# A hybrid decoder layer on one core: the front's work on PE in another order, with added matmuls of ones, and each visit's first weights traced one visit ahead

## The chip, the core and the metric

The kernel runs on one core of a Trainium2 chip. The metric is the device time of one execution in microseconds (us), as the median of 3 runs. The engines are called as in the profile: PE (TensorE, with PEld for its weight loads), DVE (VectorE), ACT (ScalarE), POOL (GpSimd) and SP (SyncE, which here issues the loads).

## What is computed

One decoder layer over 256 tokens of width 2048 in fp32, conditioned by a vector `c`. The first stage, where the change lies, is this part of the reference:

```python
mod = jax.nn.silu(c) @ w_ada[l] + b_ada[l]
shift1, scale1, gate1, shift2, scale2, gate2 = jnp.split(mod, 6, axis=-1)
h = modulate(rms_norm(x, g_norm1[l]), shift1, scale1)
p = h @ w_in[l]
```

`rms_norm` divides by the root mean square of a token and multiplies by a gain; `modulate` is h (1 + scale) + shift. Behind `p` come a retention branch and an HGRN2 branch, a merge, a second norm, a gated convolutional feed-forward and a final norm; none of them is changed.

## The kernel before

**Tiles.** Tokens are 256 columns, channels are 16 k-tiles of 128 partitions. `x` lies transposed in four tiles `xT` of four k-tiles each. A weight load (`load`, L161) brings two k-tiles by 512 columns (128x1024, 512 KB) or one (128x512) on SP's queue into one of 11 `raw` buffers. ACT rounds it to fp32r (`wh`, L176, in `upper`), DVE subtracts to get the rest (`wl`, L181, in `rest`), and PE forms a product of three: `wh` with the upper half of the activation `hT`, `wh` with its lower half, and `wl` with the upper half. `mm_cols` (L221, L222, L225) does it with weights as the stationary operand in passes of 256 columns, `mm_rows` (L205, L206, L210) with the activation as stationary in passes of 512 columns. Of the twelve column groups (`ATT`) four go by columns, eight by rows.

**The conditioning.** `mod` isn't a matmul: a row of `w_ada` transposed and its bias (2049 numbers on each of 128 partitions) is multiplied with silu(c), held on all partitions in `sc`, and summed along the row on DVE (`ada_dot`, L465, two dots of 1024 and 1025 for a scale or a shift). `scale_shift` makes from these the scale (L476, L477) and the shift (L479) of one k-tile on ACT; `modulated` makes `hT` of it (L389 and L393 on ACT, L394 on DVE). For the front `c` is loaded as two rows, spread over the partitions by four fp32 matmuls with a row of ones (L303, one active row), and passes through Silu on ACT. The squares of `x` (L372, L376) are added on DVE (L377, L378), summed over channels by matmuls of one column (L342), and a square root, a reciprocal (L352) and two matmuls (L356) give `rx`, the inverse norm of each token on all partitions; `times` (L455) multiplies it into `xT`.

**The front** (`run`, L840 to L875): for k-tile 0, then 1, the first four groups (`FIRST`, all by columns) are multiplied, with weights of one k-tile each. Groups 0 and 1 (`RESIDENT`) keep their PSUM banks until their last k-tile; the others are copied out (`take`, L835 by ACT when new, L837 added by DVE).

**Visits** (L891 on). After the front the program goes round the twelve groups. A visit brings a group as far as the k-tiles of `hT` then due: `have`, which grows by one with every `ADA_EVERY` (11) units of work, `LAG` units late. `finish` emits the steps of the due k-tiles, `products` walks through the visit's weights two k-tiles at a time (`pieces`) and lets background generators (`pump`) emit the next k-tiles' dots between. So a visit's weights are traced within the visit, and its `take` behind them.

**Order.** Up to `self.ordered = False` (L868) pinned instructions (`pin`) keep the program's order on their engine; later the scheduler of the tile layer orders each engine's instructions, which then run strictly in that order. The small attention work and the tables of sine and cosine (`trig`, L527 to L529) are spread over the visits as background.

## Time and profile before

| what | value |
|---|---|
| median of 3 runs | 1501.31 us (1500.99 to 1501.91) |
| the profiled execution's own time | 1501.3 us |
| its span, first to last instruction | 1499.5 us |
| instructions in it | 22668 |
| PE, DVE, ACT busy | 99%, 81%, 56% of the span |
| mean granted TensorE clock | 0.999 |
| read from HBM | 382.11 MB, 256 GB/s over the span |

A span of nearly the whole time means that little lies around it. Busy shares are averages over stages; what a change in a stage is worth is read there: which engine waits, for what, and what ended the wait. In rows of the timeline the first number is the start, the second the duration, both in us; `x4` are four merged instructions, and brackets tell the idle time before. A matmul's duration has its drain in it, so the pace of PE is read from start to start. An fp32 matmul stands as two passes, an fp32r one as a single pass, shown as f32.

### The profile page before, as it was taken

The numbers are of one execution on the slowest core, as the hardware profiler recorded it, in microseconds if no ns is written. First come the engines' busy times: TensorE is split into PE (matmuls) and PEld (weight loads), VectorE is DVE, ScalarE is ACT, GpSimd is POOL, SyncE is SP. The second block draws the span as 40 slices with busy tenths as digits, with TensorE's granted clock in tenths as the row PEclk, the third lists the DMA queues.
The fourth block names the chain that finished last, engine by engine and source line by source line (L and its number), as shares of the span: only waits on it lengthen the run. The fifth ranks groups of instructions, "written<-read, shape, count | busy, mean of one in ns | idle before, by whom it ended". The sixth has DMA issues, their size and how long they took to land.

```text
span 1499.5 us, 22668 instructions
## 1 busy us (share of the span) xinstructions
PE 1482.9 (99%) x8466; PEld 1268.5 (85%) x8466; DVE 1208.5 (81%) x1647; ACT 838.1 (56%) x1210; POOL 4.0 (0%) x8
## 2 busy tenths in 40 slices
PE   8999999999999999999999999999999999999997
PEld 6889899888888888888888888888888888888886
DVE  7899997998999877898978778777777769455684
ACT  5745456767775644455466556555555558344342
POOL 0000000000000000000000000000000000000000
PEclk9999999999999999999999999999999999999999
DMA  9999997778887899989847777777777666666551
GB/s 373 365 341 346 316 335 257 267 252 277 278 280 262 286 295 328 317 295 356 307 126 244 245 236 233 234 238 237 228 250 230 221 190 207 195 210 214 177 186 56
DMA packets 110994, 385.71 MB, mean 257 GB/s; under 512 B 12802, under 2 KB 13346, under 8 KB 110884
## 3 DMA queue, kind: packets, MB, share of 16 engines
q1 hardware_dynamic: 110016, 383.14, 76.6%
q8 instruction: 66, 1.08, 0.3%
q10 hardware_dynamic: 868, 1.13, 0.2%
q14 instruction: 44, 0.36, 0.1%
HBM read 382.11 MB, written 2.11 MB: 256 GB/s over the span
## 4 chain that ended last, share of the span: by engine, by line
PE 94%; DVE 2%; DMA 1%; ACT 1%; issue 1%; SPq 0%; DVEq 0%; ACTq 0%
PE pg L205 13%; PE pg L210 13%; PE pg L206 13%; PE po L1134 11%; PE pg L1134 11%; PE po L1136 5%; PE pg L1136 5%; PE pg L232 4%; PE po L205 3%; PE po L210 3%; PE po L206 3%; PE pg L235 2%; PE pg L222 1%; PE pg L221 1%; PE pg L225 1%; PE po L225 1%
## 5 line engine op out<-in xcount | busy, mean ns | idle before, releaser
L181 DVE TENSOR_TENSOR wl<-raw,wh 128x1024 fp32r<-128x1024 f32 (+1 forms) x536 | 632.8, 1191 | 222.7 <-ACT wh L176 214.1
L176 ACT ACTIVATE wh<-raw 128x1024 fp32r<-128x1024 f32 (+1 forms) x536 | 547.2, 1032 | 471.0 <-PE pg L206 196.9
L465 DVE SCALAR_TENSOR_TENSOR raw<-raw,sc 128x1024 f32<-128x1024 f32 x192 | 233.7, 1221 | 0.0
L205 PE MATMUL pg<-wh,hT 128*128 128x512 f32 x512 | 202.3, 395 | 0.9 <-DVE p L837 0.6
L206 PE MATMUL pg<-wh,hT 128*128 128x512 f32 x512 | 199.8, 390 | 0.0
L1134 PE MATMUL po<-h2T,wh 128*128 128x512 f32 x704 | 175.8, 392 | 0.0
L1134 PE MATMUL pg<-h2T,wh 128*128 128x512 f32 x688 | 172.1, 392 | 0.0
L1134 PEld LDWEIGHTS po<-h2T,wh 128*128 128x128 f32 x704 | 125.6, 188 | 21.7
L1134 PEld LDWEIGHTS pg<-h2T,wh 128*128 128x128 f32 x688 | 122.8, 188 | 21.3
L210 PE MATMUL pg<-wl,hT 128*128 128x512 f32 x512 | 138.4, 390 | 0.1
L205 PEld LDWEIGHTS pg<-wh,hT 128*128 128x128 f32 x512 | 96.1, 188 | 21.5 <-ACT f L586 1.0
L210 PEld LDWEIGHTS pg<-wl,hT 128*128 128x128 f32 x512 | 96.0, 188 | 20.6 <-DVE wl L181 0.4
L206 PEld LDWEIGHTS pg<-wh,hT 128*128 128x128 f32 x512 | 96.2, 188 | 19.6 <-DVE hT L394 0.3
L1136 PEld LDWEIGHTS po<-h2T,wl 128*128 128x128 f32 x704 | 93.4, 188 | 7.5
L1136 PEld LDWEIGHTS pg<-h2T,wl 128*128 128x128 f32 x688 | 91.4, 188 | 7.3
L1136 PE MATMUL po<-h2T,wl 128*128 128x256 f32 x704 | 94.5, 277 | 0.0
L1136 PE MATMUL pg<-h2T,wl 128*128 128x256 f32 x688 | 92.5, 277 | 0.0
L206 PE MATMUL pg<-wh,gs 128*128 128x512 f32 x176 | 68.6, 390 | 0.0
L205 PE MATMUL pg<-wh,gs 128*128 128x512 f32 x176 | 68.5, 389 | 0.0
L205 PE MATMUL po<-wh,gs 128*128 128x512 f32 x176 | 68.5, 389 | 0.0
L206 PE MATMUL po<-wh,gs 128*128 128x512 f32 x176 | 68.5, 389 | 0.0
L1147 ACT ACTIVATE u<-uy,convw 128x256 f32<-128x256 f32 x88 | 52.4, 595 | 28.7 <-DVE uy L1145 28.4
(255 smaller groups left out, 2023.9 us busy)
## 6 DMA issues: line engine op xcount, KB each, us to landing
raw<-in_wup SPq DMA_DIRECT2D x176, 512.0 KB, 4.6
raw<-in_wdown SPq DMA_DIRECT2D x88, 512.0 KB, 4.2
raw<-in_wa SPq DMA_DIRECT2D x80, 512.0 KB, 5.8
raw<-in_ada SPq DMA_DIRECT2D x64, 512.5 KB, 5.7
raw<-in_ada SPq DMA_DIRECT2D x64, 512.0 KB, 5.4
raw<-in_wab SPq DMA_DIRECT2D x64, 512.0 KB, 5.4
raw<-in_gate SPq DMA_DIRECT2D x32, 512.5 KB, 5.0
raw<-in_wk SPq DMA_DIRECT2D x32, 512.0 KB, 5.2
```

The costliest lines, as they stand in the source:

```text
L176: self.pin(self.nc.scalar.activation(wh, raw, AF.Copy))
L181: self.last = self.nc.vector.tensor_tensor(wl, raw, wh.bitcast(F32), ALU.subtract)
L205: nc.tensor.matmul(ps[t], lhsT=act[:, hi], rhs=wh, start=first and i == 0, stop=False)
L206: nc.tensor.matmul(ps[t], lhsT=act[:, lo], rhs=wh, start=False, stop=False)
L210: nc.tensor.matmul(ps[t], lhsT=act[:, hi], rhs=wl, start=False, stop=last and i == len(items) - 1)
L225: nc.tensor.matmul(outs[j], lhsT=wl[:, cs[j]], rhs=act[:, :T], start=False, stop=last and i == len(items) - 1, skip_group_check=True)
L232: nc.tensor.matmul(ps[z], lhsT=wh[:, z * P : (z + 1) * P], rhs=act, start=first and i == 0, stop=False)
L235: nc.tensor.matmul(ps[z][:, :T], lhsT=wl[:, z * P : (z + 1) * P], rhs=act[:, :T], start=False, stop=last and i == len(items) - 1)
L465: dot = self.pin(nc.vector.scalar_tensor_tensor(raw[:, 0, :], raw[:, 0, :], 1.0, self.sc[:, u * GW : u * GW + w], ALU.mult, ALU.mult, accu ...
L1134: self.pin(nc.tensor.matmul(ps[z], lhsT=wh[:, z * P : (z + 1) * P], rhs=act, start=kt == 0, stop=False, skip_group_check=bool(begun)))
L1136: nc.tensor.matmul(ps[z][:, :T], lhsT=wl[:, z * P : (z + 1) * P], rhs=act[:, :T], start=False, stop=kt == KT - 1, skip_group_check=bool(be ...
L1147: nc.scalar.activation(u, y, AF.Identity, bias=w[3], scale=w[2])
```

## The change

It rewrites the front, and moves the tracing of weights in the visits:

- `c` is loaded as 16 rows of 128 behind `ident`, turned by one transpose into a column `col`, passed through Silu once, and spread over the partitions by 16 fp32 matmuls of 128x128 (`spread`). The Silu of four row tiles becomes a Copy, and the table for the square root is loaded ahead of the squares.
- `idle` adds 21 fp32 matmuls of ones with ones, in four places (9, 1, 2 and 9), written to a PSUM tile that nothing reads.
- The last tile of squares is shared by ACT and DVE and is summed on PE without the adds on DVE.
- For k-tiles 0 and 1 the shift's dots are cut in three (1024, 512, 513). `opening` computes x times scale plus the first part on ACT, `summed` adds the other two parts on DVE; for k-tile 1 `summed` runs twice, once into the fp32r upper half.
- For k-tile 0 groups 0 and 1 multiply the loaded fp32 weights with the fp32 activation directly (`mm_plain`, four fp32 matmuls for each), without the split. For k-tile 1 `mm_apart` runs all products with the upper half first, then those with the lower half, then `wl`, over both groups.
- The first piece of visit 4 is traced in the front, and that of each later visit (`early`) before the `take` of the visit ahead of it. The plan of visits is made beforehand (`visits`). The takes of groups 2 and 3 come later, and `LAG` is 2.

```diff
-LAG = 1
+LAG = 2
...
+    def mm_plain(self, ps, w, h):
+        for j in range(4):
+            out = ps[j // 2][:, j % 2 * T : (j % 2 + 1) * T]
+            self.pin(self.nc.tensor.matmul(out, lhsT=w[:, j * P : (j + 1) * P], rhs=h, start=j % 2 == 0, stop=False, skip_group_check=True))
...
+    def mm_apart(self, pss, pieces, act):
+        nc = self.nc
+        n = range(len(pss))
+        for pick, cols in ((0, slice(0, T)), (0, slice(T, 2 * T)), (1, slice(0, T))):
+            for i in n:
+                for j in range(4):
+                    out = pss[i][j // 2][:, j % 2 * T : (j % 2 + 1) * T]
+                    w = pieces[i][pick][:, 0, j * P : (j + 1) * P]
+                    self.pin(nc.tensor.matmul(out, lhsT=w, rhs=act[:, cols], start=False, stop=False, skip_group_check=True))
...
+    def idle(self, n):
+        ps = self.pg()[0]
+        for _ in range(n):
+            self.pin(self.nc.tensor.matmul(ps[:, :P], lhsT=self.ones, rhs=self.ones, start=True, stop=True))
...
+        for step in begun or self.pieces(src[:, k0 : k0 + kts, :], kts, gain, shift):
...
-        rows = [self.blk([1, GW], name="crow") for _ in range(2)]
-        for u, row in enumerate(rows):
-            nc.scalar.dma_start(out=row, in_=a["c"][:, u * GW : (u + 1) * GW])
-        self.small_loads(nc.scalar, ("ident", "gn1"))
-        for u in range(4):
-            at = slice(u * G, (u + 1) * G)
-            ps = self.po()
-            nc.tensor.matmul(ps, lhsT=self.ones[0:1, :], rhs=rows[u // 2][:, u % 2 * G : (u % 2 + 1) * G], start=True, stop=True)
-            self.silu.append((self.sc[:, at], ps))
+        self.small_loads(nc.scalar, ("ident",))
+        row = self.blk([KT, P], name="crow")
+        self.pin(nc.scalar.dma_start(out=row, in_=a["c"]))
+        self.small_loads(nc.scalar, ("gn1",))
+        self.idle(9)
+        ps = self.po()[:, :KT]
+        self.pin(nc.tensor.transpose(ps, row, self.ident[:KT, :KT]))
+        self.idle(1)
+        col = self.small([P, KT], name="col", bufs=1)
+        self.pin(nc.scalar.activation(col, ps, AF.Silu))
+        self.sqrt_table()
+        self.col = col
+        for u in range(2):
+            self.spread(u)
+    def spread(self, u):
+        ps = self.po()
+        for i in range(4):
+            k = 4 * u + i
+            self.pin(self.nc.tensor.matmul(ps[:, i * P : (i + 1) * P], lhsT=self.col[:, k : k + 1].to_broadcast([P, P]), rhs=self.ident, start=True, stop=True))
+        self.silu.append((self.sc[:, u * G : (u + 1) * G], ps))
...
+        self.idle(2)
...
+        self.idle(9)
...
+        ps = self.po()[:, :NT]
...
             if i == 0:
                 self.pin(nc.vector.tensor_tensor(z, x, x, ALU.mult))
+            elif i < 3:
+                self.pin(nc.scalar.activation(z, x, AF.Square))
+                self.pin(nc.scalar.activation(*self.silu.pop(0), AF.Copy))
             else:
-                if i < 3:
-                    self.pin(nc.scalar.activation(*self.silu.pop(0), AF.Silu))
-                self.pin(nc.scalar.activation(z, x, AF.Square))
-            self.pin(nc.vector.tensor_tensor(z[:, :2, :], z[:, :2, :], z[:, 2:, :], ALU.add))
-            self.pin(nc.vector.tensor_tensor(z[:, 0, :], z[:, 0, :], z[:, 1, :], ALU.add))
-            parts.append(z[:, 0, :])
+                self.pin(nc.scalar.activation(z[:, :2, :], x[:, :2, :], AF.Square))
+                self.pin(nc.vector.tensor_tensor(z[:, 2:, :], x[:, 2:, :], x[:, 2:, :], ALU.mult))
+            if i < 3:
+                self.pin(nc.vector.tensor_tensor(z[:, :2, :], z[:, :2, :], z[:, 2:, :], ALU.add))
+                self.pin(nc.vector.tensor_tensor(z[:, 0, :], z[:, 0, :], z[:, 1, :], ALU.add))
+            self.sums(ps, [z[:, j, :] for j in range(1 if i < 3 else 4)], i == 0, i == 3)
+            if i == 0:
+                for u in (2, 3):
+                    self.spread(u)
...
-        if k == 0:
-            self.pin(self.nc.vector.tensor_scalar(h, x, sc[:, k : k + 1], sh[:, k : k + 1], ALU.mult, ALU.add))
-        else:
-            self.pin(act(h, x, AF.Identity, bias=sh[:, k : k + 1], scale=sc[:, k : k + 1]))
+        self.pin(act(h, x, AF.Identity, bias=sh[:, k : k + 1], scale=sc[:, k : k + 1]))
...
+    def ada_dot(self, src, cuts=(0, GW, D + 1)):
...
+        self.dots = part = self.small([P, len(cuts) - 1], name=f"dot{len(cuts)}", bufs=6 if len(cuts) == 3 else 2)
+        for u, (at, to) in enumerate(zip(cuts, cuts[1:])):
+            raw = self.load(src[:, at:to], 1, to - at)
+            dot = self.pin(nc.vector.scalar_tensor_tensor(raw[:, 0, :], raw[:, 0, :], 1.0, self.sc[:, at:to], ALU.mult, ALU.mult, accum_out=part[:, u : u + 1]))
...
+        if fine:
+            yield from self.ada_dot(self.a[name][k, 1], (0, GW, GW + G, D + 1))
+            return
...
+        def summed(dst, z, part):
+            self.pin(nc.vector.tensor_scalar(dst, z, part[:, 1:2], part[:, 2:3], ALU.add, ALU.add))
+        def first(k):
+            return self.scale_shift("ada1", k, s1, t1, self.gn1, fine=True)
+        def opening(k):
+            z = self.s1([P, T], name="z")
+            self.pin(nc.scalar.activation(z, self.xT[0][:, k, :], AF.Identity, bias=self.dots[:, 0:1], scale=s1[:, k : k + 1]))
+            return z
+        ada = [None, None, *(ada1(k) for k in range(2, KT))]
+        gen = first(0)
+        for _ in range(2):
+            next(gen)
...
+        next(gen)
+        self.times(0, 1, rx)
+        self.pin(nc.scalar.activation(rx_sb, rx, AF.Copy))
+        z = opening(0)
+        for _ in gen:
+            pass
+        h = self.s1([P, T], name="h")
+        summed(h, z, self.dots)
+        ps = {0: self.po2(), 1: self.po2()}
+        hT[0] = self.blk([P, 2, 2 * T], F32R, name="hT")
+        hi, lo = act(0)[:, :T], act(0)[:, T:]
+        plain = [self.load(a["wa"][g][:, 0:1, :], 1, G) for g in range(RESIDENT)]
+        uppers = []
+        for g in range(RESIDENT, FIRST):
+            if g == RESIDENT:
+                self.pin(nc.scalar.activation(hi, h, AF.Copy))
+            uppers.append(self.upper(a["wa"][g][:, 0:1, :], 1, G))
+        self.pin(nc.vector.tensor_tensor(lo, h, hi.bitcast(F32), ALU.subtract))
+        rests = [self.rest(z) for z in uppers]
+        self.times(1, 1, rx_sb)
+        gen = first(1)
+        for g in range(RESIDENT):
+            self.mm_plain(ps[g], plain[g][:, 0, :], h)
+        for g in range(RESIDENT, FIRST):
+            ps[g] = self.pg()
+            wh, wl = rests[g - RESIDENT]
+            mms[g](ps[g], [(act(0), wh[:, 0, :], wl[:, 0, :])], True, False)
+            for _ in range(2):
+                next(gen)
+        z = opening(1)
+        for _ in gen:
+            pass
+        uppers = [self.upper(a["wa"][g][:, 1:2, :], 1, G) for g in range(RESIDENT)]
+        hi, lo = act(1)[:, :T], act(1)[:, T:]
+        summed(hi, z, self.dots)
+        h = self.s1([P, T], name="h")
+        summed(h, z, self.dots)
+        self.pin(nc.vector.tensor_tensor(lo, h, hi.bitcast(F32), ALU.subtract))
+        rests = [self.rest(z) for z in uppers]
+        self.mm_apart([ps[g] for g in range(RESIDENT)], rests, act(1))
+        for g in range(RESIDENT, FIRST):
+            wh, wl = self.rest(self.upper(a["wa"][g][:, 1:2, :], 1, G))
+            mms[g](ps[g], [(act(1), wh[:, 0, :], wl[:, 0, :])], False, True)
+        begun = list(self.pieces(a["wa"][FIRST][:, 0:2, :], 2))
...
-            if g >= RESIDENT:
-                take(g, ps[g], True)
...
+        def visits():
+            work, g = sum(done), FIRST
+            seen = list(done)
+            while min(seen) < KT:
...
+                if m > 0:
+                    yield g, m, work
+                    seen[g] = have
+                    work += m
...
+        def early(g, m):
+            k = done[g]
+            pieces = self.pieces(a["wa"][g][:, k : k + m, :], m, shift=visit(g))
+            return chain([next(pieces)], pieces)
...
+        plan = list(visits())
+        for g in range(RESIDENT, FIRST):
+            take(g, ps[g], True)
+        for n, (g, m, work) in enumerate(plan):
...
+            fresh = done[g] == 0
+            have = done[g] + m
+            self.finish(*ada[:have])
+            bank = ps[g] if g < RESIDENT else self.pg()
+            whole = g >= RESIDENT
+            self.products(mms[g], bank, a["wa"][g], act, done[g], m, first=whole, last=whole or have == KT, shift=visit(g), begun=begun)
+            done[g] = have
+            begun = early(*plan[n + 1][:2]) if n + 1 < len(plan) else None
+            if whole or have == KT:
+                take(g, bank, fresh or not whole)
```

DVE in the front, from behind the squares' adds to the first split weights of k-tile 0. L465 (now L507) are the dots, L352 (L391) the reciprocal, L455 (L497) is `times`, L181 makes `wl`. Before:

```order
L465 SCALAR_TENSOR_TENSOR raw_142,dot_141<-raw_142,sc 128x1024
L465 SCALAR_TENSOR_TENSOR raw_145,dot_141<-raw_145,sc 128x1025
L465 SCALAR_TENSOR_TENSOR raw_151,dot_150<-raw_151,sc 128x1024
L352 RECIPROCAL rq_163<-rq_163 128x2
L465 SCALAR_TENSOR_TENSOR raw_176,dot_150<-raw_176,sc 128x1025
L455 TENSOR_TENSOR xT_95<-xT_95,po_166 128x256
L391 TENSOR_SCALAR h_187<-xT_95,s_125,t_126 128x256
L394 TENSOR_TENSOR hT_186<-h_187,hT_186 128x256
L181 TENSOR_TENSOR wl_183<-raw_180,wh_182 128x512
```

And now, where L418 is the half of the last square and L887 is `summed`:

```order
L418 TENSOR_TENSOR sq_152<-xT_116 128x512
L507 SCALAR_TENSOR_TENSOR raw_182,dot_32_181<-raw_182,sc 128x1024
L507 SCALAR_TENSOR_TENSOR raw_185,dot_32_181<-raw_185,sc 128x1025
L391 RECIPROCAL rq_191<-rq_191 128x2
L507 SCALAR_TENSOR_TENSOR raw_211,dot_39_210<-raw_211,sc 128x1024
L497 TENSOR_TENSOR xT_113<-xT_113,po_194 128x256
L507 SCALAR_TENSOR_TENSOR raw_218,dot_39_210<-raw_218,sc 128x512
L507 SCALAR_TENSOR_TENSOR raw_221,dot_39_210<-raw_221,sc 128x513
L887 TENSOR_SCALAR h_224<-z_216,dot_39_210 128x256
L923 TENSOR_TENSOR hT_230<-h_224,hT_230 128x256
L181 TENSOR_TENSOR wl_239<-raw_236,wh_238 128x512
L181 TENSOR_TENSOR wl_244<-raw_241,wh_243 128x512
```

The reciprocal moved up by one dot, the last dot of k-tile 0 is cut in two, and `wl` is made for two groups instead of four; `summed` takes the place of the affine step L391.

ACT around visits 4 and 5, the first two behind the front. L176 makes `wh`, and L835 (now L880) is the copy of `take`. Before, `wh_366` is of visit 4, `wh_392` of visit 5, and `p_133` the take of visit 4:

```order
L176 ACTIVATE wh_366<-raw_364 128x1024
L476 ACTIVATE s_125<-dot_354 128x1
L477 ACTIVATE s_125<-gn_85,s_125 128x1
L835 ACTIVATE p_131<-pg_174 128x1024
L176 ACTIVATE wh_392<-raw_390 128x1024
L835 ACTIVATE p_132<-pg_175 128x1024
L835 ACTIVATE p_133<-pg_363 128x1024
L479 ACTIVATE t_126<-dot_384 128x1
L176 ACTIVATE wh_421<-raw_419 128x1024
```

Now `wh_383` is of visit 4, `wh_418` of visit 5, `wh_441` of visit 6, and `p_173` the take of visit 4:

```order
L176 ACTIVATE wh_383<-raw_381 128x1024
L880 ACTIVATE p_171<-pg_258 128x1024
L880 ACTIVATE p_172<-pg_278 128x1024
L518 ACTIVATE s_165<-dot_77_388 128x1
L519 ACTIVATE s_165<-gn_83,s_165 128x1
L880 ACTIVATE p_173<-pg_397 128x1024
L176 ACTIVATE wh_418<-raw_416 128x1024
L176 ACTIVATE wh_441<-raw_439 128x1024
L524 ACTIVATE t_166<-dot_81_412 128x1
L880 ACTIVATE p_174<-pg_423 128x1024
```

The first weights of visit 5 stood two places ahead of visit 4's take, and now stand behind it.

ACT around the sine and cosine tables, further on among the visits (L527 to L529, now L572 to L574). Before:

```order
L176 ACTIVATE wh_1369<-raw_1367 128x1024
L527 ACTIVATE n_1238<-ang_1237 128x256
L528 ACT_TABLE_LOAD
L528 ACTIVATE sin<-ang_1237 128x256
L176 ACTIVATE wh_1405<-raw_1403 128x1024
L529 ACTIVATE cos<-n_1238,halfpi 128x256
L176 ACTIVATE wh_1438<-raw_1436 128x1024
```

And now, where `wh_1521` and `wh_1541` (one k-tile) belong to one visit and `wh_1556` is the first of the next:

```order
L176 ACTIVATE wh_1521<-raw_1519 128x1024
L176 ACTIVATE wh_1541<-raw_1539 128x512
L572 ACTIVATE n_1353<-ang_1352 128x256
L573 ACT_TABLE_LOAD
L573 ACTIVATE sin<-ang_1352 128x256
L574 ACTIVATE cos<-n_1353,halfpi 128x256
L176 ACTIVATE wh_1556<-raw_1554 128x1024
L524 ACTIVATE t_166<-dot_253_1508 128x1
```

A copy of weights stood between sine and cosine, and the block had a piece of two k-tiles ahead of it; now the block is unbroken and has a piece of one k-tile ahead of it. Likewise, some 40 us earlier, a `t<-dot` (L524, a shift, which waits for DVE's dot) now stands right ahead of a visit's first weights, `wh_1097`.

116 lines of the change are left out of this document (37 added, 79 removed).

## The prediction

> **What bounds the kernel now.** I read the page first, then the windows of the first 60 us, PE's waits, and the timeline of each engine in the front.
>
> ```profile
> span 1499.5 us, 22668 instructions
> PE 1482.9 (99%) x8466; PEld 1268.5 (85%) x8466; DVE 1208.5 (81%) x1647; ACT 838.1 (56%) x1210; POOL 4.0 (0%) x8
> ...
> 0.00:10.00 10.00, 7.75 (x11) 3.15 (x12) 4.44 (x12) 5.16 (x6) 0.20 (x4) 1.00 0.83 281
> 10.00:20.00 10.00, 6.59 (x29) 6.21 (x30) 9.41 (x19) 7.11 (x15) 0.00 (x0) 1.00 1.03 407
> 20.00:30.00 10.00, 8.78 (x65) 8.38 (x64) 9.67 (x17) 4.87 (x10) 0.00 (x0) 1.00 1.03 407
> 30.00:40.00 10.00, 9.78 (x55) 8.36 (x54) 7.68 (x12) 7.73 (x12) 0.00 (x0) 1.00 1.03 405
> 40.00:60.00 20.00, 20.00 (x89) 16.29 (x88) 16.60 (x24) 14.70 (x21) 0.00 (x0) 1.00 1.03 408
> ```
>
> PE is busy for 99% of the span and has no gap from 40 us. So a change to the front is worth what it does to the moment from which PE is dense, plus what it does to PE's waits later; nothing else shows in the end. DVE, with over 9 of 10 us busy between 10 and 30, sets the pace of the front, and the loads run without a pause (share 1.03, 407 GB/s, so 1.29 us for 512 KB).
>
> PE's useful work starts at 17.55, with the first k-tile. The second starts at 26.34, and visit 4, the first of 512 columns, at 33.04; from there PE is dense:
>
> ```profile
> 17.55 0.80 PE L221 MATMUL po<-hT,wh 128*128 128x256 f32 x2 [1.20 <-ACT hT L389]
> ...
> 26.34 0.74 PE L221 MATMUL po<-hT,wh 128*128 128x256 f32 x4 [1.01 <-ACT hT L389]
> ...
> 33.04 0.50 PE L205 MATMUL pg<-wh,hT 128*128 128x512 f32 x1 [0.22 <-ACT p L835]
> ```
>
> In the front PE also runs at two paces, though the granted clock reads 1.00 throughout. A 128x256 pass takes 0.22 us up to 20.95 and 0.12 from 21.6:
>
> ```profile
> 2.25 7.16 PE L303 MATMUL po<-crow,ones 1*128 1x512 f32 x8 [2.25 <-DMA crow<-in_c]
> 9.34 3.57 PE L342 MATMUL po<-ones,sq 128*128 128x1 f32 x16
> 15.13 1.22 PE L356 MATMUL po<-ident,rq 128*128 128x128 f32 x4 [2.21 <-DVE rq L352]
> ...
> 20.73 0.41 PE L221 MATMUL po<-hT,wh 128*128 128x256 f32 x1
> 20.95 0.41 PE L222 MATMUL po<-hT,wh 128*128 128x256 f32 x1
> ...
> 22.06 0.28 PE L221 MATMUL pg<-hT,wh 128*128 128x256 f32 x1
> 22.18 0.28 PE L222 MATMUL pg<-hT,wh 128*128 128x256 f32 x1
> ```
>
> The fast pace came 3.9 us after the dense matmuls began at 17.55. 7.16 us of matmuls with one active row (L303) and 16 passes of one column (L342) did not bring it: L356 is still slow. The Trainium skill, "TensorE: Matmul & The Clock Gate", section "Part 1: The HAM clock gate", says that about 3.4 us of sustained activity doubles the clock, in a window that runs freely, and that an idle window takes it back. The 3.9 us agree; L303 does not, if any running instruction counts as activity. By the rule at its word the front of before would have been fast by 9 us; the sum goes by the rows.
>
> **The change, part by part.** *First k-tile.* Work now waits on DVE. Its steps:
>
> ```profile
> 9.18 0.69 DVE L377 TENSOR_TENSOR sq<-sq 128x512 f32<-128x512 f32 x1 [1.34 <-ACT sq L376]
> ...
> 14.91 0.17 DVE L352 RECIPROCAL rq<-rq 128x2 f32<-128x2 f32 x1
> ...
> 17.87 2.49 DVE L181 TENSOR_TENSOR wl<-raw,wh 128x512 fp32r<-128x512 f32 x4
> ...
> 21.42 0.42 DVE L455 TENSOR_TENSOR xT<-xT,po 128x256 f32<-128x256 f32 x1
> 21.75 1.22 DVE L465 SCALAR_TENSOR_TENSOR raw<-raw,sc 128x1025 f32<-128x1025 f32 x1
> ...
> 22.90 1.22 DVE L465 SCALAR_TENSOR_TENSOR raw<-raw,sc 128x1024 f32<-128x1024 f32 x1
> ```
>
> From start to start a dot costs 1.15 us, a 128x512 operation 0.60 (four in 2.49), a 128x256 one 0.33; half a dot, which no row shows, lies between 0.33 and 1.15, and I take the 0.60 of the same width. The third x-tile's square ends on ACT at about 9.6, against 9.16 (DVE's 9.18 row): the table load of L402 now stands ahead of the squares, and ACT has little air there. Then DVE does 0.60 + 0.33 (adds), 0.60 (half of the last square), 2 x 1.15, 0.09, 1.15, 0.33 (times), 2 x 0.60, 0.42 (sum): 16.65, and some 0.4 of hand-overs: the first dense matmul at 17.05, 0.5 earlier. The reciprocal that PE's `rx` waits for now stands behind two dots, not three, and the adds on the last square are gone.
>
> PE has 108 passes of fp32 ahead of that point (21 idle, 16 spreading, 14 sums, 2 of `rx` and a transpose, two passes each). At 0.107 us, half of the fp32 pass of 256 columns below, they take about 12 us of the 16; the dense start at about 1 us puts the fast pace at 5 to 8. With that the nine idle matmuls end at about 16.4 and cover nothing that PE needs.
>
> *Plain groups.* Two groups take fp32 instead of three fp32r products: 8 matmuls of two passes at 0.214,
>
> ```profile
> 461.03 1.02 PE L758 MATMUL po<-p,p 128*128 128x256 f32 x4
> ```
>
> (1.02 less the last one's 0.378, over three). 16 x 0.214 = 3.42 against 24 x 0.12 = 2.9 of before: +0.5 us of PE work, but it lies in front of a wait. PE: 17.05 + 3.42 + 24 x 0.115 for the other two = 23.25.
>
> *Second k-tile.* DVE from 17.05: 1.0 to the end of `lo` (behind a 0.60 copy on ACT), 2 x 0.60, 0.33, 3 x 1.15, 2 x 0.60, 0.42: 24.7, PE at 24.9. PE idles 1.7 us before, which nothing fills. Then 48 passes x 0.115 = 5.5 follow; the activations and weights of each come 0.3 to 1 us ahead of it. Visit 4 starts at 30.4 (its weights now stand ahead of the third k-tile's dots on SP): **2.6 us** earlier. Bounds: 2.0 (another 0.6 of hand-overs), 3.0 (fast by 5 us and a half dot at 0.5).
>
> *Visit 5.* Here the order of ACT decides (its rows stand in the section on the change): the take of visit 4, `p_173<-pg_397`, now stands ahead of `wh_418`, the first weights of visit 5; of before `wh_392` stood two places ahead of the take. ACT is in order, so `wh_418` waits until visit 4 is through, though its load has landed: 11.0 MB go ahead of it and with it, 2.8 MB of them by 10 us and 0.407 per us after, which makes 30.2, and even two us more would be early enough.
>
> ```profile
> 29.33 1.06 ACT L176 ACTIVATE wh<-raw 128x1024 fp32r<-128x1024 f32 x1 [2.03 <-DMA raw<-in_wa]
> ...
> 33.84 1.01 ACT L835 ACTIVATE p<-pg 128x1024 f32<-128x1024 f32 x1
> ```
>
> Visit 4 ends at 30.4 + 12 x 0.227 + 0.17 of drain = 33.3; the take 1.0, the copy 1.06, hand-overs 0.05: PE begins visit 5 at 35.4, where it could at 33.1. **2.25 us** lost, bounds 2.0 and 2.4. Behind the take also stand `wh_441` and a `t`; DVE waits for `wh_418` with `wl_419`, which costs nothing more.
>
> *Later visits.* PE's waits of before between 40 and 300 us sum to about 1.9 us, start to start against 0.115 or 0.227 a pass (and 0.1 of slow start behind each):
>
> ```profile
> 118.52 0.28 PE L221 MATMUL po<-hT,wh 128*128 128x256 f32 x1
> 118.87 0.50 PE L210 MATMUL pg<-wl,hT 128*128 128x512 f32 x1
> ...
> 127.08 0.28 PE L222 MATMUL po<-hT,wh 128*128 128x256 f32 x1
> 127.43 0.74 PE L225 MATMUL po<-hT,wl 128*128 128x256 f32 x4
> ...
> 272.25 0.63 PE L210 MATMUL pg<-wl,hT 128*128 128x512 f32 x2
> 273.51 0.47 PE L205 MATMUL pg<-wh,hT 128*128 128x512 f32 x1 [0.64 <-DVE p L837]
> ```
>
> These places are reordered, so I count them as gone. Two new ones come. The sine and cosine block stands unbroken on ACT behind a piece of one k-tile, 1.36 us of PE:
>
> ```profile
> 131.43 0.40 ACT L527 ACTIVATE n<-ang 128x256 f32<-128x256 f32 x1
> 131.85 1.28 ACT L528 ACT_TABLE_LOAD   x1
> 133.14 0.42 ACT L528 ACTIVATE sin<-ang 128x256 f32<-128x256 f32 x1
> ...
> 134.42 0.49 ACT L529 ACTIVATE cos<-n,halfpi 128x256 f32<-128x256 f32 x1
> ```
>
> It is 2.6 us long and 3.6 with the copy behind it; PE has 1.36 and what is left of the piece before. Between 0 and 2.3 us; I take 1.2. And a `t<-dot` stands ahead of the first weights of a visit near 103 us; it waits for DVE's dot, one step of 1.15 and a tile's add in front of it: between 0 and 2.3, I take 1.0, near one dot.
>
> *At nothing:* the takes of groups 2 and 3 (1.0 us each on ACT) move behind the second k-tile and lie beside visit 4; were they not hidden, visit 4 would start one take later. LAG regroups the visits, with as many passes and some adds more or fewer on DVE, beside dense matmuls. `c` as 16 rows is 8 KB, and lands with the first x-tile; a microsecond more would shift ACT's squares, and the front, by as much.
>
> Sum: -2.6 + 2.25 + 2.2 - 1.9 = -0.05. The profiled execution took 1501.3 (1499.5 of span, 1.8 around it) and the median of the runs is 1501.31, so no correction: **1501.2**. All bounds low: -3.0 + 2.0 - 1.9 = -2.9; all high: -2.0 + 2.4 + 4.6 - 1.9 = +3.1. The middle of these, 1499.2 to 1503.4, is the forecast's own range.
>
> **The rivals.** *The front's gain is kept* (0.13): the take finds visit 4 done, or visit 5's copy is hidden, as `wh_392` was. For it: ACT is only 56% busy. Against it: an engine's order is fixed, and only 2.7 us of PE lie between the two. -2.6, and the later waits cancel: 1498.5, half of it under 0.2%, with the waits gone 1496.8.
>
> *Idle matmuls of ones do not bring the fast pace* (0.09), the case on the other side. The 108 passes then take 0.2135 each, 23.1 us, and the first useful matmul comes at 24.0, not 17.05. PE is then the bound of the front: 24.0 + 3.4 + 2.8 = 30.2 at the second k-tile, 5.4 late: 1506.6. It turns slower than 0.2% as soon as the 108 passes last over 16 us, that is, with a slow pace to beyond 9 us. Against it: these have 128 active rows, as the matmuls at 17.55 had.
>
> *The pace falls back* between 10 and 14 us (0.08), where PE has only one-column sums, which did not count in L342. The sums, `rx` and four of the nine idle ones run at 0.21; the first useful matmul comes at 18.8: +1.8, 1503.0. No row here has a dense stretch with such a pause behind it. The Trainium skill's rule of the idle window (same page and section) speaks for it, and would give this time.
>
> **How the numbers follow.** Forecast 0.70. 0.2% is 3.0 us, about what a measurement tells from no change. Faster by more: 0.08, of the kept gain. Slower by more: 0.09 of the slow pace and 0.03 of the fall-back, 0.12. Within: 0.80. The range 1498.6 to 1504.4 takes in the forecast, half of the kept gain and most of the fall-back.
>
> **What would show it.** Right: two passes of an idle matmul in 0.21 us by 8 us, first plain matmul at 17.0 to 17.2, the first 128x512 matmul at 30 to 31, then a wait of 2 us near 35 ended by ACT's wh. Wrong: plain passes at 0.43, visit 4 after 32, or visit 5 without a wait.

## The result, and the profile after

| | before | after |
|---|---|---|
| median of 20 runs each, on one chip | 1501.53 us (1500.99 to 1502.83) | 1503.62 us (1503.05 to 1507.21) |
| the profiled execution's own time | 1501.3 us | 1503.57 us |
| its span | 1499.5 us | 1501.8 us |

The ratio is 1.0016 [1.0009, 1.0022]: 2.1 us slower by the medians, where 1501.2 was forecast. The difference is inside 0.2%, but its interval excludes equality. Eleven of the twenty runs lie between 1503.05 and 1503.67; the others are scattered above, at a mean granted clock of up to 0.4% less. Among the experiments below, one execution of e_fill took 5319 us, far from all others, and is left out of its ratio.

The page of the changed kernel, and the windows of its first 60 us (length, then busy time and instructions of PE, PEld, DVE, ACT and POOL, then granted clock, DMA share and GB/s):

```profile
span 1501.8 us, 22826 instructions
PE 1485.5 (99%) x8537; PEld 1274.6 (85%) x8537; DVE 1210.5 (81%) x1654; ACT 839.8 (56%) x1211; POOL 4.0 (0%) x8
...
0.00:10.00 10.00, 7.97 (x55) 7.74 (x56) 3.66 (x10) 5.33 (x8) 0.20 (x4) 1.00 0.81 284
10.00:20.00 10.00, 9.37 (x62) 8.97 (x62) 9.00 (x20) 5.25 (x12) 0.00 (x0) 0.83 1.03 397
20.00:30.00 10.00, 9.22 (x70) 8.81 (x69) 9.80 (x21) 4.73 (x8) 0.00 (x0) 1.00 1.04 404
30.00:40.00 10.00, 7.94 (x41) 6.51 (x41) 7.57 (x12) 6.42 (x9) 0.00 (x0) 1.00 1.03 408
40.00:60.00 20.00, 20.00 (x90) 16.56 (x89) 15.71 (x22) 15.51 (x23) 0.00 (x0) 1.00 1.01 386
```

PE is now busy between 10 and 20 us, where it had been 6.59, and has a hole between 30 and 40, where it had been 9.78. PE's timeline shows the hole, and the places further on where it waits:

```profile
6.16 2.05 PE L339 MATMUL po<-ident,col 128*128 128x128 f32 x16
...
18.43 3.62 PE L231 MATMUL po<-h,raw 128*128 128x256 f32 x16
...
25.69 2.14 PE L242 MATMUL po<-hT,wh 128*128 128x256 f32 x16 [0.78 <-ACT wh L176]
...
31.51 0.40 PE L205 MATMUL pg<-wh,hT 128*128 128x512 f32 x1
...
36.48 0.50 PE L205 MATMUL pg<-wh,hT 128*128 128x512 f32 x1 [2.06 <-ACT wh L176]
...
104.69 0.50 PE L205 MATMUL pg<-wh,hT 128*128 128x512 f32 x1 [0.56 <-ACT wh L176]
...
150.97 1.20 PE L210 MATMUL pg<-wl,hT 128*128 128x512 f32 x4 [0.25 <-DVE wl L181]
...
280.35 0.47 PE L205 MATMUL pg<-wh,hT 128*128 128x512 f32 x1 [0.58 <-DVE p L882]
...
287.89 0.47 PE L205 MATMUL pg<-wh,hT 128*128 128x512 f32 x1 [0.46 <-DVE p L882]
```

**Where the 2.3 us of span come from.** Visit 4 starts at 31.51 against 33.04: -1.53. PE then loses 2.33 ahead of visit 5 (from start to start), where it lost about nothing: +2.33. Between 40 and 300 us I summed PE's gaps again, from start to start less the pace, in both traces: 2.42 before, 3.86 after, +1.44. Together +2.2. Beyond 300 us the two run alike: the changed kernel is 2.1 us behind at 345 us and 2.3 at the end.

| place (us) | before | after | read as |
|---|---|---|---|
| 41, 118, 127 | 0.99 | 0 | gone, as counted |
| 272, 274 / 280, 288 | 1.22 | 1.56 | still there: PE waits for DVE's add `p` |
| 103 to 105 | 0 | 0.95 | new: `t<-dot` ahead of `wh` |
| 148 to 151 | 0 | 0.91 | new: 0.33 of `wh` behind the sine and cosine block, 0.54 of `wl` behind an add on DVE |

(The rest, 0.21 and 0.44, lies in pieces under 0.2 us and of 0.13 at 167. Such sums hold many small pieces and are good to about 0.1.)

Visit 5 on ACT, in the timeline of the changed kernel: the take `p` begins when visit 4 is done, and the copies `wh` follow it.

```profile
34.46 1.02 ACT L880 ACTIVATE p<-pg 128x1024 f32<-128x1024 f32 x1 [0.80 <-PE pg L210]
35.38 2.00 ACT L176 ACTIVATE wh<-raw 128x1024 fp32r<-128x1024 f32 x2
```

The load of the first `raw` had landed by 32.7, so nothing but the place behind the take held its copy.

And the wait at 104.69, on ACT, DVE and PE:

```profile
100.99 1.22 DVE L882 TENSOR_TENSOR p<-p,pg 128x1024 f32<-128x1024 f32 x1
...
102.13 1.22 DVE L507 SCALAR_TENSOR_TENSOR raw<-raw,sc 128x1025 f32<-128x1025 f32 x1
...
103.39 0.29 ACT L524 ACTIVATE t<-dot 128x1 f32<-128x1 f32 x1 [4.91 <-DVE raw L507]
...
103.59 1.04 ACT L176 ACTIVATE wh<-raw 128x1024 fp32r<-128x1024 f32 x1
...
104.69 0.50 PE L205 MATMUL pg<-wh,hT 128*128 128x512 f32 x1 [0.56 <-ACT wh L176]
```

The add at 100.99 takes up what PE finished just before, the dot follows the add, `t` the dot, `wh` stands behind `t`, and PE waits for `wh`. So the chain begins at PE itself: when PE comes earlier, the whole chain and its wait come earlier with it. The larger part of the wait near 151 is of the same kind: DVE sits idle for PE, does the add, and only then makes the `wl` that PE waits for, though its `wh` was done by 148.5.

```profile
148.56 1.22 DVE L882 TENSOR_TENSOR p<-p,pg 128x1024 f32<-128x1024 f32 x1 [0.70 <-PE pg L210]
149.70 2.35 DVE L181 TENSOR_TENSOR wl<-raw,wh 128x1024 fp32r<-128x1024 f32 x2
```

### The profile page after: what moved, and what is told of

It is laid out like the page before. It is cut to its first block, busy times and chain, and to the rows that moved or that the text cites. A ratio compares the mean times of both kernels' runs of the same rounds, so it can differ in the third digit from the quotient of the medians.

```text
span 1501.8 us, 22826 instructions
## 1 busy us (share of the span) xinstructions
PE 1485.5 (99%) x8537; PEld 1274.6 (85%) x8537; DVE 1210.5 (81%) x1654; ACT 839.8 (56%) x1211; POOL 4.0 (0%) x8
## 4 chain that ended last, share of the span: by engine, by line
PE 90%; DVE 5%; ACT 2%; DMA 1%; issue 1%; DVEq 0%; ACTq 0%; SPq 0%
PE pg L205 12%; PE pg L210 12%; PE pg L206 12%; PE po L1231 11%; PE pg L1231 11%; PE po L1233 5%; PE pg L1233 5%; PE pg L255 4%; PE po L206 3%; PE po L205 3%; PE po L210 3%; DVE wl L181 2%; PE pg L258 2%; DVE raw L507 1%; DVE p L882 1%
## 5 line engine op out<-in xcount | busy, mean ns | idle before, releaser
L181 DVE TENSOR_TENSOR wl<-raw,wh 128x1024 fp32r<-128x1024 f32 (+1 forms) x535 | 631.2, 1190 | 225.4 <-ACT wh L176 217.2
L176 ACT ACTIVATE wh<-raw 128x1024 fp32r<-128x1024 f32 (+1 forms) x535 | 545.8, 1032 | 468.1 <-PE pg L206 185.2
L507 DVE SCALAR_TENSOR_TENSOR raw<-raw,sc 128x1024 f32<-128x1024 f32 (+2 forms) x194 | 233.5, 1209 | 0.0
```

What stands on the lines that cost most here:

```text
L176: self.pin(self.nc.scalar.activation(wh, raw, AF.Copy))
L181: self.last = self.nc.vector.tensor_tensor(wl, raw, wh.bitcast(F32), ALU.subtract)
L507: dot = self.pin(nc.vector.scalar_tensor_tensor(raw[:, 0, :], raw[:, 0, :], 1.0, self.sc[:, at:to], ALU.mult, ALU.mult, accum_out=part[:, ...
```

## The experiments

Every run is timed in five rounds beside the kernel before on the same chip. "Later waits" are PE's gaps between 40 and 300 us in its profile.

| run | median us | ratio to before | visit 4 at | wait at visit 5 | later waits |
|---|---|---|---|---|---|
| after, again (e_after) | 1503.48 | 1.0016 [1.0008, 1.0025] | 31.30 | 2.33 | 3.87 |
| e_hold | 1501.60 | 1.0006 [0.9997, 1.0015] | 32.56 | 0.37 | 3.87 |
| e_wide | 1503.73 | 1.0021 [1.0011, 1.0030] | 32.91 | 2.33 | 3.87 |
| e_front | 1504.37 | 1.0021 [1.0011, 1.0030] | 32.57 | 2.22 | 3.99 |
| e_visits | 1500.92 | 1.0002 [0.9993, 1.0010] | 33.52 | 0.04 | 3.03 |
| e_table | 1501.31 | 1.0000 [0.9991, 1.0009] | 30.73 | 0.93 | 3.86 |
| e_noidle | 1503.63 | 1.0015 [1.0007, 1.0024] | 32.65 | 0.21 | 3.86 |
| e_fill | 1501.40 | 1.0000 [0.9991, 1.0009] | 32.76 | 0.36 | 3.88 |
| e_lag1 | 1501.48 | 1.0003 [0.9994, 1.0012] | 30.93 | 0.93 | 3.91 |
| e_oldvisits | 1501.41 | 1.0002 [0.9993, 1.0011] | 32.32 | 0.36 | 3.81 |
| e_trig | 1502.28 | 1.0005 [0.9996, 1.0014] | 32.24 | 0.19 | 3.80 |
| e_idle11 | 1501.39 | 1.0002 [0.9993, 1.0011] | 31.29 | 0.37 | 3.83 |
| e_noadd | 1502.56 | 1.0011 [1.0003, 1.0020] | 30.88 | 0.78 | 4.94 |
| e_order | 1503.08 | 1.0016 [1.0007, 1.0025] | 30.87 | 0.93 | 5.37 |
| e_best | 1503.30 | 1.0015 [1.0006, 1.0024] | 30.66 | 0, at visit 6 1.69 | 4.79 |
| e_one | 1502.38 | 1.0008 [0.9999, 1.0017] | 31.14 | 0.68 | 4.78 |
| e_both | 1502.42 | 1.0008 [0.9999, 1.0017] | 31.34 | 0.67 | 4.74 |

The columns on the right are each from one profiled execution, and these vary in the front: e_table and e_trig have the same front, and their visit 4 starts at 30.73 and 32.24. The ratios are the firmer column.

### The wait at visit 5

**e_hold** puts the take of visit 4 behind the first copy of visit 5 on ACT:

```diff
-                    nc.scalar.activation(dst, z, AF.Copy)
+                    ins = nc.scalar.activation(dst, z, AF.Copy)
+                    if behind is not None:
+                        self.tc.add_manual_dep(ins.ins, behind.ins.name, NOSYNC, reason="behind the first weights of the next visit")
...
-                take(g, bank, fresh or not whole)
+                take(g, bank, fresh or not whole, self.rounded if begun is not None and (n == 0) else None)
```

> ACT takes the first weights of visit 5 ahead of the copy (take) of visit 4; nothing else moves on PE, and on ACT only a tiny t<-dot. Theory: the whole 2.2 us that PE waits at 34.0 in the kernel after come from this order, since the load of these weights has landed by 32.7, before visit 4 ends at 34.3. Then visit 5 follows visit 4 without a gap, and the time is 2.2 us below the kernel after: 1501.4. Rival: the loads, which run without a pause up to 47 us, are the limit behind; PE that arrives 2.2 us earlier then waits as long for weights between 37 and 48, and the time stays at 1503.6.

```profile
34.47 1.04 ACT L176 ACTIVATE wh<-raw 128x1024 fp32r<-128x1024 f32 x1
35.50 1.03 ACT L880 ACTIVATE p<-pg 128x1024 f32<-128x1024 f32 x1
```

```profile
35.57 0.50 PE L205 MATMUL pg<-wh,hT 128*128 128x512 f32 x1
```

The two have changed places, PE's wait falls from 2.33 to 0.37, and the ratio from 1.0016 to 1.0006: about 1.5 us by the ratios, with visit 4 a microsecond later in this profile. Beside e_wide (below), which keeps the wait and ran on the same chip, it is 2.1 us. The rival, that the loads take the gain back, fell: the later waits stay at 3.87.

**e_front** takes the new front with `LAG` 1, and the pieces traced within their visit from visit 5 on (visit 4's first piece is still traced in the front).

```diff
-LAG = 2
+LAG = 1
...
-            begun = early(*plan[n + 1][:2]) if n + 1 < len(plan) else None
+            begun = None
```

> The new front alone: behind visit 4 each visit's weights are traced within the visit again and LAG is 1. Theory: the front gains its 1.5 us (visit 4 at 31.5 against 33.0), but ACT still takes the copy of visit 4 ahead of the first weights of visit 5, so the wait of 2.2 us near 34 stays, as it comes from the front's timing and not from the tracing; the later waits are like those of before, 1.9 us. Sum +0.7 on before's 1501.5: 1502.2. Rival: the wait comes from tracing ahead; without it visit 5 follows without a gap, and the front's gain stands: 1500.0.

The wait at visit 5 stays at 2.2 without tracing ahead. So it comes with the front, with which that take stands ahead of visit 5's weights on ACT, and not with the later early pieces. The rest of the expectation missed: the later waits are 3.99, not 1.9, and the median is 1504.37, not 1502.2. In its profile the granted clock also falls, from 37.5 to 40.9 (shown at the end).

**e_visits** is the other half: the front of before, with `visits`, `early`, the later takes and `LAG` 2.

> The old front with the new visits: first pieces traced a visit ahead, takes of groups 2 and 3 behind visit 4's first piece, LAG 2. Theory: the first k-tile at 17.55 and visit 4 at 33.0 as before, no wait at visit 5 (ACT has its first weights ahead of the copy of visit 4), and later waits up to 300 us of some 3.4 us as in the kernel after instead of 1.9: +1.5, 1503.0. Rival: the new visits cost nothing by themselves, the later waits of the kernel after come from its earlier front: 1501.5, with 1.9 us of waits.

No wait at visit 5, later waits 3.03, level with before. The time is that of the rival (1501.5), not the 1503.0 of the theory. The new visits alone cost nothing that can be measured in the time, though 0.6 us of waits are added.

### The front

**e_table** is e_hold with the load of the square root's table moved behind the squares and copies on ACT:

```diff
         self.pin(nc.scalar.activation(col, ps, AF.Silu))
-        self.sqrt_table()
...
+        self.sqrt_table()
```

> With ACT's order at visit 5 turned (as in e_hold), and the load of the square root's table put behind the squares and copies, where ACT waits anyway. Theory: the table load of 1.28 us ahead of the squares makes the third tile's adds on DVE start at 10.0 instead of 9.2; with it moved they start at 9.2, DVE's chain and visit 4 come 0.6 to 0.8 us earlier, 1500.9 if e_hold is at 1501.6. Rival: the tiles of x or the spreading on PE hold the squares as long, and nothing moves: 1501.6.

First ACT and DVE of the changed kernel, then DVE and PE of e_table:

```profile
6.12 1.28 ACT L402 ACT_TABLE_LOAD   x1
...
7.53 1.04 ACT L414 ACTIVATE sq<-xT 128x1024 f32<-128x1024 f32 x1
...
10.03 0.69 DVE L420 TENSOR_TENSOR sq<-sq 128x512 f32<-128x512 f32 x1 [0.28 <-ACT sq L414]
```

```profile
8.85 0.69 DVE L419 TENSOR_TENSOR sq<-sq 128x512 f32<-128x512 f32 x1 [0.28 <-ACT sq L413]
...
24.85 2.20 PE L242 MATMUL po<-hT,wh 128*128 128x256 f32 x16 [1.07 <-DVE hT L887]
...
34.30 0.50 PE L205 MATMUL pg<-wh,hT 128*128 128x512 f32 x1 [0.66 <-ACT wh L176]
```

DVE's adds on the third tile start 1.18 earlier, nearly the whole table load, the second k-tile 0.84 and visit 4 0.78 earlier. (Other profiles differ by some tenths: 10.12 in e_after and 10.18 in e_hold with the load ahead, 9.19 in e_lag1 without.) About 0.6 of it is given back at visit 5 (0.93 against 0.37), whose copy stands behind a scale on ACT that waits for DVE's dot. Against before: -2.31 + 0.93 + 1.43 = +0.05, and its span is 1499.5, that of before. It is 2.2 us below the changed kernel on the same chip, and level with before.

**e_noidle** is e_hold without the 21 matmuls of ones.

> With ACT's order at visit 5 turned, and without the 21 added matmuls of ones. Theory: they bring the fast pace by 4 to 10 us; without them the spreading, the sums and rx run at 0.21 us a pass, rx and so DVE's chain come later, the plain groups may still be slow, and visit 4 comes at 33 or later: 1 to 2 us above e_hold, 1502.6 to 1503.6. Rival: DVE's chain is the bound at either pace and the added matmuls bring nothing: 1501.6.

```profile
18.23 5.96 PE L231 MATMUL po<-h,raw 128*128 128x256 f32 x16 [2.44 <-DVE h L883]
```

Without them the plain groups take 5.96 instead of 3.62, and the ratio is 1.0015 against 1.0006 for e_hold: the ones are worth some 1.4 us by the ratios, whose intervals overlap. The two profiles do not show it: their second k-tiles start at 26.89 and 26.74 and visit 4 at 32.65 and 32.56, as in the one of e_hold the fast pace came only past 10 us, and the one of e_noidle is of a run 1.1 us below its median.

**e_wide** gives the sums of squares 128 columns instead of one, so that PE works at full width between 10 and 14 us.

```diff
-                        ps[:, t : t + 1],
+                        ps[:, t * P : (t + 1) * P],
...
-                        rhs=self.ones[:, 0:1],
+                        rhs=self.ones,
```

> The sums over channels take all 128 columns of ones instead of one, as many passes, and each token's sum stands 128 times beside itself. Theory: the granted clock fell to 0.50 from 14.2 to 17.6 us because the 3.4 us ahead of that held little but one-column sums; with 128 columns it stays at 1.00 from its first rise on. DVE then gets rx 0.33 earlier, the first plain matmul comes at 17.5 instead of 18.4, and visit 4 at 31.2 instead of 31.5, since DVE's chain bounds the second k-tile: 1503.3, and the runs lie closer together than 1503.0 to 1507.2. Rival 1: the clock carries the whole miss of the front, and visit 4 comes at 30.4 as forecast: 1502.5. Rival 2: what lowers the clock is not the sums; it falls to 0.50 again near 14 us, visit 4 stays at 31.5, 1503.6.

The granted clock no longer fell there, and the plain groups began at 17.23 instead of 18.43. The time did not improve: its fastest run is 1503.07, that of the changed kernel 1503.05. In its profile the clock fell behind the next pause instead (length, PE, PEld, DVE, ACT, POOL, clock, DMA share, GB/s):

```profile
23.00:26.55 3.55, 1.77 (x15) 1.60 (x15) 3.41 (x10) 2.74 (x6) 0.00 (x0) 1.00 1.05 408
26.55:29.96 3.41, 3.41 (x18) 3.41 (x18) 2.51 (x5) 1.65 (x2) 0.00 (x0) 0.50 1.03 411
```

**e_fill** is e_table with the wide sums, and five fp32 matmuls that add zero ahead of the second k-tile; **e_idle11** is e_fill with 11 instead of 9 matmuls of ones at the start.

```diff
+        for _ in range(5):
+            self.pin(nc.tensor.matmul(ps[0][0][:, :P], lhsT=self.zeros, rhs=self.ones, start=False, stop=False, skip_group_check=True))
```

> All at once: ACT's order at visit 5 turned, the table load behind the squares, sums of 128 columns, and five fp32 matmuls that add zero ahead of the second k-tile, where PE waits 0.8 to 1.9 us for DVE. Theory: each of the falls of the granted clock seen so far (at 14.2, 26.6, 37.5) follows a window of 3.4 us in which PE did little; with those places filled the clock stays at 1.00 from its first rise to the last visits, visit 4 comes at 30.6, and the median lies within 0.3 us of the fastest run: 1500.4, 0.5 below before on this chip. Rival: the falls come at random or from load, they stay, and the median lies 0.5 us or more above the fastest run, as in the kernel after.

> As e_fill, with 11 added matmuls at the start instead of 9. In three profiles out of seven with the nine the granted clock rose only at 10.2 to 10.6, where PE's pause between 4.9 and 5.6 (nine done, c not landed) lay in the window ahead; visit 4 then came at 32.6 instead of 31.4. Theory: two more close that pause, the clock rises by 6.9 at the latest, and no run lies 1 us above the fastest; median 1501.2 where before is at 1501.5. Rival: the two stand in front of the transpose of c and delay sc by 0.4, and the time goes up by as much.

Neither profile shows a fall of the clock. With nine ones its first rise can still come late: in the profile of e_fill, as in that of e_hold, the fast pace came only past 10 us, and visit 4 at 32.76 against 31.29 in e_idle11. The medians stay those of e_table, so the gains of 0.5 and 0.3 below before that were expected did not come. But the eleven runs of e_idle11 lie between 1501.10 and 1501.76, 0.66 us apart, where the twenty of the changed kernel spread over 4.2. Two kernels further down have the same wide sums, fill and 11 ones: the runs of e_best lie 0.50 apart and those of e_both 0.47, where e_order and e_one, without them, have 1.47 and 1.22. So these edits together narrow the spread, while the median stays (1502.42 for e_both, 1502.38 for e_one on the same chip).

**e_after** is the changed kernel again, as a control.

> The kernel after, unchanged, beside the others on one chip. Theory: 2.0 to 2.7 us above before, and 2.1 us above the same kernel with ACT's order at visit 5 turned. A second profile of it shows whether the granted clock falls at the same place (14.2 to 17.6): if it follows a window that runs freely against the start, it falls elsewhere or not at all, and visit 4 comes between 31.2 and 32.9 with it.

The clock fell from 14.76 to 18.17 in it, elsewhere than before, and `times` came at 15.34 all the same, right behind DVE's dot: no loss.

### The later waits

**e_lag1** is e_table with `LAG` 1. **e_oldvisits** also traces the pieces within their visit from visit 6 on. **e_trig** is e_table with the sine and cosine work started earlier (`SMALL` 60 instead of 70).

> As e_table (ACT's order at visit 5 turned, table load behind the squares), with LAG 1 instead of 2. PE's waits between 40 and 300 us sum to 3.8 us in the kernel after and in e_table, to 2.4 before. Theory: LAG decides where they fall; with 1 a copy of weights stands between sine and cosine again as before, the sum goes back to about 2.4, and the time to 1.4 below e_table (1500.1 where before is at 1501.5). Rival: the tracing a visit ahead makes them, and the sum stays near 3.8, the time at e_table's.

> As e_lag1, and from visit 6 on each visit's weights are traced within the visit again, as before the change. If the tracing ahead makes the extra waits between 40 and 300 us, this and not e_lag1 falls to 2.4 us of waits, 1.4 below e_table. If LAG makes them, both do. If the earlier front makes them, neither does, and both stay at e_table's time.

> As e_table, with the tables of sine and cosine begun at 60 units of work instead of 70. On ACT the block then has two pieces of two k-tiles ahead of it instead of one of one k-tile. Theory: the block of 2.6 us starves PE only because the piece ahead of it is short; PE's waits near 146 to 150 us (0.9 in all) go, no new ones come at the block's new place, and the time is 0.9 below e_table. Rival: a block of 2.6 us costs PE about the same wherever it stands: e_table's time.

Each moves waits, and none lowers their sum by more than 0.1. In e_trig the one near 148 is gone, and 0.39 at 134 and 0.26 at 165 are new. In e_lag1 one of 1.24 stands near 41, since a dot stands ahead of the lower half of `hT` on DVE:

```profile
41.57 0.50 PE L206 MATMUL pg<-wh,hT 128*128 128x512 f32 x1 [1.08 <-DVE hT L436]
```

What e_front, e_lag1 and e_oldvisits share with the changed kernel is the new front, and by the test that the expectation of e_oldvisits set, the front brings the higher sum, not `LAG` or the tracing ahead. The places differ from one to the next, and the rows don't show how the front does it. Why the sum returns to 3.8 or 3.9 each time stays open; it may be chance.

**e_noadd** is e_table without the adds of three takes, to see whether DVE's load (40 adds for 37) makes the waits.

```diff
-            if whole or have == KT:
+            if (whole or have == KT) and n not in (11, 12, 13):
```

> As e_table, but the adds of three takes on DVE (groups 3, 4 and 5 in their second visit, near 75 to 83 us) are left out, so these groups lack the part of those k-tiles. Theory: DVE, with 0.9 us of idle time between 80 and 180 us against 2.6 before, is what ends the waits of PE near 102 and 147; LAG 2 gives it 40 adding takes against 37, and without three of them the waits between 80 and 175 us fall from 2.0 to 1.0 or less, the time by 1.0 or more below e_table. Rival: these waits come from the order on ACT (a t<-dot and the sine block ahead of weights); ACT's order stays here, the waits stay at 0.72 and 0.9, and the time at e_table's.

The sum rose to 4.94, so the forecast missed. But it does not settle what DVE's load does: the wait near 148 shrank to 0.2, while ACT's order changed, which the rival had held fixed. Near 102 `hT` and `h` now stand ahead of `wh` on ACT, and a wait of 1.02 at 168 is new, ended by DVE's `wl`; together they cost more than was saved:

```profile
102.20 0.49 PE L205 MATMUL pg<-wh,hT 128*128 128x512 f32 x1 [0.25 <-ACT hT L434]
...
103.64 0.50 PE L205 MATMUL pg<-wh,hT 128*128 128x512 f32 x1 [0.94 <-ACT wh L176]
```

**e_order** (all dots behind the lower half of `hT`) and **e_one** (only the first such dot) try to remove the wait of e_lag1 near 41. **e_best** adds to e_order, and **e_both** to e_one, the wide sums, the fill and the 11 ones; e_best also brings the weights of visits 5 and 6 forward. The edit of e_one against e_lag1:

```diff
-        self.pin(self.nc.vector.tensor_tensor(dst[:, T:], h, dst[:, :T].bitcast(F32), ALU.subtract))
+        ins = self.pin(self.nc.vector.tensor_tensor(dst[:, T:], h, dst[:, :T].bitcast(F32), ALU.subtract))
+        self.lower = ins if self.lower is None else False
...
+            if self.lower:
+                self.tc.add_manual_dep(dot.ins, self.lower.ins.name, NOSYNC, reason="behind the lower half of k-tile 2")
+                self.lower = False
```

> As e_lag1, with each dot on DVE behind the lower half of hT that was traced ahead of it; near 40 us the lower half of k-tile 2 then stands ahead of a dot of 1.15 us, not behind it. Theory: the upper halves are ready at 40.3 (h on ACT), the wait of PE near 41 falls from 1.24 to 0.3 to 0.4, and the time is 0.9 below e_lag1. Rival: the loads of that k-tile set it, DVE waits for h instead, and what is gained at 41 returns at the next wait: e_lag1's time.

> e_order with the first weights of visit 5 traced ahead of visit 4's products and ahead of the scale of k-tile 2 on ACT, visit 6's weights ahead of visit 5's copy, sums of 128 columns, 11 added matmuls at the start and five of zeros ahead of the second k-tile. Theory: the wait at visit 5 falls from 0.8 to 0.2 or less, that at 41 to 0.4, and the clock doesn't fall: 1.4 below e_lag1, 0.7 below before. Rival: as PE comes earlier, the loads (no pause up to 60 us) hold it in 40 to 60, and the time is e_lag1's, 0.5 above before.

> As e_lag1, with a single dot (the first of k-tile 3) held behind the lower half of k-tile 2 on DVE, where e_order held all dots. Theory: only the wait near 41 changes, from 1.24 to 0.5, as in e_order, and the waits behind it stay at e_lag1's (2.4 from 60 to 300 us): 0.75 below e_lag1, level with before or 0.1 under it. Rival: the order that the scheduler makes of the rest changes with it, and new waits take the 0.75 back.

> e_one with sums of 128 columns, 11 added matmuls at the start and five of zeros ahead of the second k-tile. Theory: the waits behind 60 us are those of e_one to within 0.1 us each, as they hang on the order and not on when the front ends; the runs lie closer together (within 0.7 us, as in e_idle11), and the median is 0 to 0.3 below e_one's. Rival: PE waits less behind a front that ends later and more behind one that ends earlier, and the two kernels differ in their later waits by what their fronts differ.

None gains on e_lag1. Against before on their own chips e_order and e_best are 2.2 and 2.5 us slower; e_one and e_both are 1.2 slower, and their intervals overlap with that of e_lag1 (0.6 slower). In e_one 41's wait falls from 1.24 to 0.48, and 0.78 at 72 and 0.43 near 102 are new; in e_order it is 1.25 near 102. In e_best visit 5's wait went to visit 6. The later waits of e_both equal those of e_one to 0.03 us each, though its front is another (visit 4 comes 0.2 later):

```profile
72.01 0.39 PE L222 MATMUL po<-hT,wh 128*128 128x256 f32 x1 [0.62 <-DVE hT L436]
```

```profile
72.21 0.39 PE L222 MATMUL po<-hT,wh 128*128 128x256 f32 x1 [0.62 <-DVE hT L438]
```

**The wait near 103 over the kernels that keep the changed kernel's order.** Its row reads `[0.56 <-ACT wh L176]` in after, e_after, e_hold, e_wide, e_table, e_noidle, e_fill, e_trig and e_idle11, at starts from 102.51 (e_table, visit 4 at 30.73) to 106.09 (e_wide, visit 4 at 32.91 and the wait at visit 5 behind it). A row of e_table:

```profile
102.51 0.50 PE L205 MATMUL pg<-wh,hT 128*128 128x512 f32 x1 [0.56 <-ACT wh L176]
```

The 3.6 us between them change nothing in it. The order of the engines sets this wait, not the moment at which PE arrives. No version here is clearly faster than before; which order would be stays open.

## Why the prediction was wrong, point by point

The front, visit 5 and the new waits had the right signs. The 2.4 us between the forecast and the median come from two places of the sum: 1.1 from the later waits, where some were counted as gone, and 1.1 from the front. The median of 1503.62 lies above the forecast's own range, 1499.2 to 1503.4, and inside the wider one, 1498.6 to 1504.4; the change stayed inside 0.2%, as was given 0.80. What did not hold is that gains and losses cancel.

**"These places are reordered, so I count them as gone": this step failed.** It was right for the waits at 41, 118 and 127 (0.99). The pair at 272 and 274 was no property of the place: PE waits there for DVE's add, which empties its PSUM tile, and that pair came back at 280 and 288 with 1.56. In e_visits and e_table, with `LAG` 2 as well, it is there too; with `LAG` 1 it is where it was before, and as long. A row of e_table, and one of e_lag1:

```profile
278.17 0.47 PE L205 MATMUL pg<-wh,hT 128*128 128x512 f32 x1 [0.59 <-DVE p L884]
```

```profile
273.75 0.47 PE L205 MATMUL pg<-wh,hT 128*128 128x512 f32 x1 [0.64 <-DVE p L884]
```

The forecast had 2.2 - 1.9 = +0.3 between 40 and 300 us; +1.44 was measured, although before's waits were 2.42 by the full sum, which speaks the other way. The 3.86 of the changed kernel are the two new waits (1.86, where 2.2 was forecast), the pair (1.56, where nothing was) and 0.44 of small waits, for which the forecast had none.

**The front, -2.6: right mechanism, wrong size; -1.53 was measured, below the bound of 2.0.** The squares' end on ACT was put at 9.6, and was 10.03: the table load of 1.28 stood in their way nearly whole, where 0.42 was allowed for it. That start, 0.43 late, is about half of the 0.79 by which the second k-tile missed (25.69, where 24.9 was forecast); `times`, which waited 0.33 for `rx` in this profile, makes up most of the rest. In e_after it did not wait, and the second k-tile came at 25.48. e_table, without the load there, has it at 24.85, but partly by chance: its adds start 0.75 ahead of the forecast's 9.6, and its chain on DVE is as much longer than forecast. From the second k-tile to visit 4, 5.82 instead of 5.5: 48 passes at 0.121, not 0.115. 0.8 + 0.3 is the 1.1 that was missing. The nine ones behind `rx` were to end at 16.4 and cover nothing; at the lowered clock they ran until 18.43, where the first plain matmul follows them without a gap, 0.7 after its `h` was ready. That cost nothing further on, as DVE sets the second k-tile.

**Visit 5, +2.25: right.** 2.33, ended by ACT's `wh` behind the take; e_hold takes it away.

**Two new later waits, 1.2 + 1.0: right in place and size, half right in mechanism.** 0.91 at 148 to 151 and 0.95 at 103 to 105. ACT's rows near 148 show the block as forecast, with the copy behind it and PE at 148.58. But that is 0.33 of the 0.91; most of the rest stands behind an add on DVE, of which the forecast says nothing, so that the size of the first term is in part luck:

```profile
145.46 1.28 ACT L573 ACT_TABLE_LOAD   x1
146.75 0.42 ACT L573 ACTIVATE sin<-ang 128x256 f32<-128x256 f32 x1
147.08 0.50 ACT L574 ACTIVATE cos<-n,halfpi 128x256 f32<-128x256 f32 x1
147.48 1.04 ACT L176 ACTIVATE wh<-raw 128x1024 fp32r<-128x1024 f32 x1
```

**At nothing:** held in the time. e_visits and e_lag1 price the new visits and `LAG` within the measurement, though `LAG` decides where the later waits fall.

**The rival of the slow ones:** fell. In the changed kernel's profile the pace is fast from the spreading on, 2.05 for its first 16 passes, and the plain passes took 0.215, as forecast. It is not so in every run: in the profile of e_hold the same 16 passes took 3.62.

**The rival of the falling pace:** its mechanism happened, its price did not. PE's windows show the fall (columns as above):

```profile
10.79:14.21 3.42, 2.89 (x24) 2.75 (x24) 3.42 (x8) 1.55 (x5) 0.00 (x0) 1.00 1.02 381
14.21:17.62 3.41, 3.32 (x16) 3.32 (x16) 3.05 (x8) 1.45 (x4) 0.00 (x0) 0.50 1.05 404
```

It was to cost 1.8. But DVE's chain bounded the front: `times` at 15.56 waited 0.33 for `rx`, and in e_after not at all; the later plain groups end ahead of the second k-tile's wait. e_wide, without that fall, has the second k-tile at 25.59, where the two with it have 25.69 and 25.48. The price is 0 to 0.3 us. That the 1503.0 of this rival lies near the measured time is chance.

**The kept gain** fell with visit 5's wait, as its counter-argument said. (Its 1498.5 should read 1498.7, which is 1501.3 less 2.6.)

**The signs.** The fast pace by 8 us and the wait near 35 behind ACT's `wh` came as named. The first plain matmul at 18.43 and visit 4 at 31.51 came after the times named for right, and visit 4 ahead of the 32 named for wrong.
